# A state-space front rewritten: output tables as two products summed by TensorE, tables in the order of the rounds, eight modulation blocks moved behind it

## The chip, the cores and the metric

The kernel runs on one core of a Trainium2 chip. The metric is the device time of one execution in microseconds (us). The engines are TensorE (PE in the profile; PEld is its weight load), VectorE (DVE), ScalarE (ACT), GpSimd (POOL) and SyncE (SP), whose queue issues most of the DMAs.

## The reference

The input is one sequence of 512 tokens of width 1024 in float32, and a conditioning vector `c`. Four layers follow one another: a state-space mixer with a gated feed-forward, a short convolution with a gated feed-forward, dilated attention with a squared-ReLU feed-forward, and a gated recurrence with another. The change is in the first mixer and its surroundings:

```python
c_act = silu(c)
mods = c_act @ w_ada[i] + b_ada[i]              # 6 x 1024: sh1, sc1, g1, sh2, sc2, g2
h = rms_norm(x, norm1_g[i]) * (1 + sc1) + sh1
# 64 groups g of 16 channels, 64 complex states each
state_t = Abar_g * state_{t-1} + Bbar_g @ u_t   # Abar = exp((a_re + i a_im) * exp(log_step))
y_t = Re(C_g @ state_t) + D * u_t
x = x + g1 * (val * sigmoid(gate))              # [val, gate] = gelu(y) @ w_out
h = rms_norm(x, norm2_g[i]) * (1 + sc2) + sh2   # then the gated feed-forward
```

## The kernel before, in words

The first part, `s5()`, which this text calls the front, computes the mixer up to the GELU. A sequence of 512 tokens is cut into 64 chunks of 8. Inside a chunk the recurrence is a dense matrix, between chunks it is a scan. Everything is laid out by `f`, one of eight blocks of eight groups, and by `i`, one of four rounds of two blocks.

The front first makes, on VectorE, the discretised poles from `a_re`, `a_im` and `log_step` (arrays of 128 x 64), their powers 0 to 8 (`pre_`, `pim_`), and the scaled `B` (`b1`, `b2`) and `C` (`c1`, `c2`), the second of each pair being the first with its halves swapped by a matmul with a permutation (`io_matrices`). Then come tables. `tables(f)` makes `w1 = b1*pre_ + b2*pim_`, three VectorE operations of 128 x 1024, the middle one into `w1t` (for f = 1 and 4 on GpSimd); eight matmuls turn `w1` into `bt` (from inputs to chunk states) and into entries of `X`, the response inside a chunk. `out_tables(f)` makes `ft = c1*pre_ - c2*pim_`, from chunk states to outputs, in two halves of three GpSimd operations, with four buffers for `ft`.

A round `i` has these parts. `prep(i)` normalises the tokens into `U` and makes rotation factors `sr`, `cr` and the scan's decay `d0` (`sr` and `d0` on GpSimd for f < 5, on VectorE else). `states(i)` copies 16 groups of `X` into the block-triangular `TT` by eight DMAs on SP's queue, multiplies `U` by `bt` (L673), rotates, scans over 64 chunks (`tensor_tensor_scan`, L688), rotates back and writes `sp`, of which there are two buffers. `outs(i)` sums `U` by `TT` (L711) and `sp` by `ft` (L713) in PSUM, copies to `Y`, transposes, applies the GELU and splits the result into a rounded part `hhi` and a rest `hlo`.

Among these stand the first 20 of 24 blocks of layer 0's modulation: `ada` loads 1 MB of `w_ada` over SP into one of three `raw` buffers, and runs eight TensorE matmuls with `c_act` as weights (L241), a ScalarE copy, and two small matmuls (L247). The rest of the modulation, 4 blocks of layer 0 and 24 of layer 1, is done after the front by `ada_fill`: the same load, then one VectorE scaling (L277) and seven multiply-adds (L279), and for every four blocks a few small matmuls. These closures stand in a list, `fillers`; `pump()` runs one whenever the matmul loops `run` and `up` have loaded a weight block, 36 times up to the end of the convolution's input projection, where the rest is run at once.

The order of the front's parts is written by hand as a string of letters: T `tables`, O `out_tables`, P `prep`, S `states` (three steps), Y `outs` (two), A `ada`, K `setup` (token loads, `X`'s diagonal, identity copies), B `io_matrices`, Q and G scales and gains, Z and H pools. A scheduler assigns each engine's instruction order from the order of that program text and from when buffers come free; at run time each engine works in order.

After the front every matrix product runs as three float32r matmuls (L849 to L851): rounded weights by rounded input, rounded weights by the rest, rest of the weights by rounded input. `gain[0, 4]`, the second norm's factor `norm2_g * (1 + sc2)`, and `mod(0, 3)`, its shift, are read when the first projection is done, by `rms_to_h`.

Of the kernel before, what the change touches and what calls it, by code (L numbers as in the profile page):

```python
# [92 lines left out]
def body(ctx, tc, a, out):  # L93
# [275 lines left out]
    ORDER = ("A1 A1 K0 A1 A1 B0 T2 Q0 A1 Z0 O0 O4 A1 G0 T5 O2 T6 G1 T3 T0 A1 O1 A1 T1 P0 A1 T4 O5 O3 S0 A1 A1 "  # L369
             "P1 T7 A1 P2 S0 S1 S1 S0 Y0 H0 S2 A1 S2 S1 P3 A1 S2 Y0 O6 Y1 S3 A1 O7 S3 S3 A1 A1 Y1 Y2 Y2 Y3 Y3 "  # L370
             "A20")
    FA, FD = 5, 5

    def s5():

        def tiny(nm, n=64, pool=p1):
            return pool.tile([128, n], F32, name=nm)

        pt = pst("b")
# [49 lines left out]
        dt = exp(lg, "e0")  # L429
        mag = exp(tt(tiny("lrdt"), lr, dt), "e1")  # L430
        th = red2pi(tt(tiny("lidt"), li, dt), "t1")
# [9 lines left out]
        tt(pre_[:, 1, :], mag, cs)  # L441
        tt(pim_[:, 1, :], mag, sn)
        tmp = p1.tile([128, 4, 64], F32, name="pw_t")
        n = 1
        while n < 8:
            br = pre_[:, n:n + 1, :].to_broadcast([128, n, 64])
            bi = pim_[:, n:n + 1, :].to_broadcast([128, n, 64])
            src_r, src_i = pre_[:, 1:n + 1, :], pim_[:, 1:n + 1, :]
            dr, di = pre_[:, n + 1:2 * n + 1, :], pim_[:, n + 1:2 * n + 1, :]
            t = tmp[:, 0:n, :]  # L450
            tt(dr, src_r, br)
            tt(t, src_i, bi)
            tt(dr, dr, t, OP.subtract)
            tt(di, src_r, bi)
            tt(t, src_i, br)
            tt(di, di, t, OP.add)
            n *= 2
# [5 lines left out]
        V.reciprocal(den, den)  # L463
        am1 = tiny("am1")
# [13 lines left out]
        T2P = (1, 4)  # L478
        more = list(range(20))
# [10 lines left out]
        th8 = tiny("th8")  # L490
        V.tensor_scalar(th8, th, 8.0, None, op0=OP.mult)
        w8 = red2pi(th8, "t8")
        w8p = tiny("w8p", pool=pp)
        V.tensor_scalar(w8p, w8, 1.0 / (2 * math.pi), None, op0=OP.mult)
        w8 = w8p
        r8 = tiny("r8", pool=pp)
        tt(r8, mag, mag)
        tt(r8, r8, r8)
        tt(r8, r8, r8)


        b1, b2 = (pt1.tile([128, 64, 16], F32, name=nm) for nm in ("b1", "b2"))
        c1, c2 = (pp.tile([128, 64, 16], F32, name=nm) for nm in ("c1", "c2"))
        X = pp.tile([128, 64, 16], F32, name="X")
        TT = [pp.tile([128, 8, 16, 16], F32, name=f"TT{i}") for i in range(2)]
# [8 lines left out]
        def tables(f):  # L514
            g = slice(8 * f, 8 * f + 8)
            w1 = pt1.tile([128, 8, 8, 16], F32, name="w1", bufs=2)
            t2 = pt1.tile([128, 8, 8, 16], F32, name="w1t", bufs=1)
            tt(w1, b1[:, g, None, :].to_broadcast([128, 8, 8, 16]), bc(pre_, slice(0, 8), g))
            (P if f in T2P else V).tensor_tensor(t2, b2[:, g, None, :].to_broadcast([128, 8, 8, 16]),
                                                 bc(pim_, slice(0, 8), g), op=OP.mult)  # L520
            tt(w1, w1, t2, OP.add)
            ic = IC[f % 2]
            A.copy(ic[:, :, 128:144], c1[:, g, :])
            bt = pp.tile([128, 8, 128], F32, name=f"bt{f}")
            for g0, n in ((0, 3), (3, 3), (6, 2)):
                p = pst("c", (128, 3, 144))
                for j in range(n):
                    T.matmul(p[:, j], w1[:, g0 + j].rearrange("p l h -> p (l h)"), ic[:, g0 + j], start=True, stop=True)
                A.copy(bt[:, g0:g0 + n], p[:, 0:n, 0:128])
                gx = slice(8 * f + g0, 8 * f + g0 + n)  # L530
                tt(X[:, gx], X[:, gx], p[:, 0:n, 128:144], OP.add)
            Bt[f] = bt

        def out_tables(f):
            g = slice(8 * f, 8 * f + 8)
            ft = pp.tile([128, 8, 8, 16], F32, name="ft", bufs=4)
            for i in range(2):
                gs = slice(8 * f + 4 * i, 8 * f + 4 * i + 4)
                fi = ft[:, 4 * i:4 * i + 4]
                ft2 = pp.tile([128, 4, 8, 16], F32, name="ft2", bufs=1)  # L540
                P.tensor_tensor(fi, c1[:, gs, None, :].to_broadcast([128, 4, 8, 16]), bc(pre_, slice(1, 9), gs), op=OP.mult)
                P.tensor_tensor(ft2, c2[:, gs, None, :].to_broadcast([128, 4, 8, 16]), bc(pim_, slice(1, 9), gs), op=OP.mult)
                P.tensor_tensor(fi, fi, ft2, op=OP.subtract)  # L543
            Ft[f] = ft

        def io_matrices(_):
# [17 lines left out]
            for dst, src, tag in ((c2, c1, "a"), (b2, b1, "b")):  # L564
                for j in range(2):
                    p = pst(tag, (128, 32, 16))
                    T.matmul(fl(p), C("sw"), fl(src[:, hf[j]]), start=True, stop=True)
                    A.activation(dst[:, hf[j]], p, AF.Identity, scale=C("sg"))


        def setup(_):
            load_chunks()

            P.memset(X, 0.0)
            P.tensor_tensor(X[0:16], drow, C("e")[0:16, None, :].to_broadcast([16, 64, 16]), op=OP.mult)
            for ic in IC:
                A.copy(ic[:, :, 0:128], ident[:, None, :].to_broadcast([128, 8, 128]))
            for t in TT:
                P.memset(t, 0.0)

# [17 lines left out]
        def gains(h):  # L598
            ada_next(max(0, 4 * h + 4 - (20 - len(more))))
# [33 lines left out]

        def prep(i, st):
# [67 lines left out]
        def outs(i, st):  # L702
            U = st["U"]
            Y = ps2.tile([128, 8, 8, 16], F32, name="Y", bufs=1)
            for j in range(2):
                p = pst("c", (128, 4, 8, 16))
                for q in range(4):
                    gi = 4 * j + q
                    for s in range(2):
# [3 lines left out]
                        T.matmul(o, st["sp", s][:, gi, 0:64], Ft[2 * i + s][:, gi], start=False, stop=True,  # L713
                                 tile_position=(0, 64 * s))
# [24 lines left out]
        def open_h(_):  # L739
# [8 lines left out]
              "H": open_h, "B": io_matrices, "K": setup, "Q": token_scale, "G": gains, "Z": open_2}  # L748
# [10 lines left out]
    make_gain(0, 4, "norm2_g")  # L759
# [306 lines left out]

    ada_fill(0, 40, 48)
# [726 lines left out]
```

## Time and profile before

| | |
|---|---|
| median of 3 runs | 2768.0 us (2766.3 to 2771.34) |
| the profiled execution's own time | 2767.48 us |
| its span in the profile | 2765.7 us |
| mean granted TensorE clock | 0.989 of full speed |
| busy over the span | PE 2694.6, DVE 1565.3, ACT 1068.6, POOL 123.5 us |

The span runs from the first instruction to the last; 1.8 us of the time lie around it. An engine's busy time says how much it did, not whether anyone waited for it. Where the profile gives a stretch's granted clock, 1.00 stands for 2.4 GHz and 0.50 for 1.2 GHz.

### The profile page before, as it was taken

To read this page: it belongs to the slowest core of one execution; us is meant where nothing else is said; L and a number is where in the kernel's file an instruction comes from. 1 tells how busy PE (TensorE), PEld (TensorE's weight loads), DVE (VectorE), ACT (ScalarE), POOL (GpSimd) and SP (SyncE) were. 2 spreads that over 40 slices of the span, in tenths; PEclk is the share of its full clock that TensorE was granted. 3 is DMA by queue.
4 is the path that set the end of the run, shared out by engine and by line. 5 is a ranking of instruction groups with operands and counts; after the bars stand their busy time and mean duration, and the time that the engine had idled before them with its cause. 6 is when DMAs were issued, how large, how long until landed. Compare 5 with 4: busy or idle time off the path is not lost.

```text
span 2765.7 us, 37495 instructions
## 1 busy us (share of the span) xinstructions
PE 2694.6 (97%) x15356; PEld 2286.1 (83%) x15356; DVE 1565.3 (57%) x2803; ACT 1068.6 (39%) x1874; POOL 123.5 (4%) x123
## 2 busy tenths in 40 slices
PE   5889999999999999999999999999999999999998
PEld 3668988889889888898888888898888988988887
DVE  8767755547555333375555555664446766744436
ACT  4653422224334222254343344452323666432322
POOL 7420000000000000000000000000000000000000
PEclk8989999999999999999999999999999999999999
DMA  6547445432332233343332333222224212223221
GB/s 191 163 132 243 153 137 176 146 128 84 122 107 98 86 99 106 100 120 93 91 99 85 92 94 90 62 88 96 91 84 130 82 61 66 88 92 103 88 84 61
DMA packets 301008, 298.18 MB, mean 108 GB/s; under 512 B 9748, under 2 KB 287252, under 8 KB 300836
## 3 DMA queue, kind: packets, MB, share of 16 engines
q1 hardware_dynamic: 292660, 279.37, 31.4%
q10 hardware_dynamic: 5840, 10.05, 1.4%
q0 software_dynamic: 2336, 6.36, 1.0%
q8 instruction: 121, 1.98, 0.3%
q14 instruction: 51, 0.42, 0.0%
HBM read 278.71 MB, written 2.10 MB: 102 GB/s over the span
## 4 chain that ended last, share of the span: by engine, by line
PE 90%; DVE 4%; ACT 3%; DMA 1%; POOL 1%; issue 1%; SPq 0%; DVEq 0%; ACTq 0%; POOLq 0%
PE ps_mm L849 24%; PE ps_mm L850 24%; PE ps_mm L851 24%; PE ps_mm L862 2%; PE ps_mm L863 2%; PE ps_mm L864 2%; PE ps_sc L1322 1%; PE ps_pt L1349 1%; PE ps_b L673 1%; PE ps_mm L1224 1%; ACT whi L803 1%; POOL ft L543 1%; PE ps_mm L1226 1%; PE ps_x L241 1%; PE ps_mm L1225 1%
## 5 line engine op out<-in xcount | busy, mean ns | idle before, releaser
L849 PE MATMUL ps_mm<-hhi,whi 128*128 128x512 f32 (+1 forms) x2064 | 786.5, 381 | 0.0
L850 PE MATMUL ps_mm<-hlo,whi 128*128 128x512 f32 (+1 forms) x2064 | 782.6, 379 | 0.5 <-DVE hlo L359 0.5
L851 PE MATMUL ps_mm<-hhi,wlo 128*128 128x512 f32 (+1 forms) x2064 | 781.2, 378 | 0.5 <-DVE wlo L804 0.5
L803 ACT CAST whi<-raw 128x1024 fp32r<-128x1024 f32 (+1 forms) x428 | 414.0, 990 | 819.5 <-PE ps_mm L850 628.8
L804 DVE TENSOR_TENSOR wlo<-raw,whi 128x1024 fp32r<-128x1024 f32 (+1 forms) x428 | 485.4, 1151 | 380.6 <-ACT whi L803 350.4
L849 PEld LDWEIGHTS ps_mm<-hhi,whi 128*128 128x128 f32 x2064 | 387.8, 188 | 73.7 <-issue 3.1
L851 PEld LDWEIGHTS ps_mm<-hhi,wlo 128*128 128x128 f32 x2064 | 388.0, 188 | 72.6 <-DVE wlo L804 1.0
L850 PEld LDWEIGHTS ps_mm<-hlo,whi 128*128 128x128 f32 x2064 | 387.9, 188 | 70.4 <-DVE hlo L359 0.9
L850 PE MATMUL ps_mm<-hidl,whi 128*128 128x512 f32 (+1 forms) x1120 | 401.5, 359 | 0.0
L849 PE MATMUL ps_mm<-hidh,whi 128*128 128x512 f32 (+1 forms) x1120 | 401.3, 359 | 0.1
L851 PE MATMUL ps_mm<-hidh,wlo 128*128 128x512 f32 (+1 forms) x1120 | 400.8, 358 | 0.0
L850 PEld LDWEIGHTS ps_mm<-hidl,whi 128*128 128x128 f32 x1120 | 211.0, 188 | 31.2
L849 PEld LDWEIGHTS ps_mm<-hidh,whi 128*128 128x128 f32 x1120 | 210.3, 188 | 31.3 <-ACT hidh L358 0.3
L851 PEld LDWEIGHTS ps_mm<-hidh,wlo 128*128 128x128 f32 x1120 | 210.4, 188 | 31.0
L1172 DVE TENSOR_TENSOR xT<-xT,ps_mm 128x512 f32<-128x512 f32 (+1 forms) x128 | 71.7, 567 | 121.8 <-PE ps_mm L851 121.1
L862 PE MATMUL ps_mm<-hhi,whi 128*128 128x256 f32 x448 | 123.9, 281 | 1.0 <-ACT hq L1581 0.6
L863 PE MATMUL ps_mm<-hhi,wlo 128*128 128x256 f32 x448 | 124.4, 279 | 0.0
L864 PE MATMUL ps_mm<-hlo,whi 128*128 128x256 f32 x448 | 124.2, 280 | 0.2
L358 ACT CAST hidh<-silu 128x512 fp32r<-128x512 f32 (+1 forms) x124 | 68.9, 565 | 126.0 <-DVE silu L996 83.0
L957 DVE SCALAR_TENSOR_TENSOR xT<-ps_mm,mods,xT 128x512 f32<-128x512 f32 (+1 forms) x104 | 64.8, 625 | 92.6 <-PE ps_mm L851 92.5
L279 DVE SCALAR_TENSOR_TENSOR ada_acc<-raw,c_act,ada_acc 128x256 f32<-128x256 f32 x196 | 93.5, 483 | 4.9
L1273 POOL DMA_DIRECT2D qsw<-qc x48 | 23.4, 492 | 1564.4 <-ACT qc L1262 1550.5
(414 smaller groups left out, 3386.3 us busy)
## 6 DMA issues: line engine op xcount, KB each, us to landing
raw<-in_w_ada_dram SPq DMA_DIRECT2D x48, 1024.0 KB, 5.2
raw<-in_w_ffn_in_dram SPq DMA_DIRECT2D x44, 1024.0 KB, 4.9
raw<-in_ffn_w_up_dram SPq DMA_DIRECT2D x32, 1024.0 KB, 5.2
raw<-in_attn_w_in_dram SPq DMA_DIRECT2D x48, 512.0 KB, 4.7
raw<-in_ffn_w_down_dram SPq DMA_DIRECT2D x32, 768.0 KB, 4.3
raw<-in_w_ffn_out_dram SPq DMA_DIRECT2D x24, 768.0 KB, 4.3
raw<-in_conv_w_in_dram SPq DMA_DIRECT2D x12, 1024.0 KB, 5.0
raw<-in_attn_w_in_dram SPq DMA_DIRECT2D x12, 1024.0 KB, 4.8
```

Of the source, the lines that this page charges most:

```text
L279: V.scalar_tensor_tensor(ac, raw[:, k, :], c_act[:, k:k + 1], ac, op0=OP.mult, op1=OP.add)
L358: A.copy(hi, src)
L803: A.copy(hi[:, sl], raw[:, sl])
L804: V.tensor_tensor(lo[:, sl], raw[:, sl], hi[:, sl].bitcast(F32), op=OP.subtract)
L849: T.matmul(ps[:, 0:n], hi[:, k, cs], h, start=(k == 0), stop=False)
L850: T.matmul(ps[:, 0:n], hi[:, k, cs], l, start=False, stop=False)
L851: T.matmul(ps[:, 0:n], lo[:, k, cs], h, start=False, stop=(k == nk - 1))
L862: T.matmul(p[:, 0:n], hi[:, k, cs], h, start=(k == 0), stop=False)
L863: T.matmul(p[:, 0:n], lo[:, k, cs], h, start=False, stop=False)
L864: T.matmul(p[:, 0:n], hi[:, k, cs], l, start=False, stop=(k == nk - 1))
L957: V.scalar_tensor_tensor(x, ps, gcol[:, m:m + 1], x, op0=OP.mult, op1=OP.add)
L1172: V.tensor_tensor(x, x, ps, op=OP.add)
```

## The change

The output table of a block is kept as its two products `fa` and `fb`, two buffers each; the sign goes into `c2`, and TensorE sums by a second matmul on the same `sp`. GpSimd keeps only these 32 products, a small memset and copy, and one load. VectorE makes every `w1t` and `sr` and `X`'s diagonal, and clears `X` and `TT` first of all; ScalarE copies `d0`. The powers above the first become a step W of the order, after `io_matrices`, and small steps ahead of them change places. In the order, two tables precede round 0, and the others stand among the rounds. `ada` makes 12 blocks instead of 20; the eight for the second norm's shift and scale become fillers, ahead of all others, and the last of them makes `gain[0, 4]`.

```diff
-    ORDER = ("A1 A1 K0 A1 A1 B0 T2 Q0 A1 Z0 O0 O4 A1 G0 T5 O2 T6 G1 T3 T0 A1 O1 A1 T1 P0 A1 T4 O5 O3 S0 A1 A1 "
-             "P1 T7 A1 P2 S0 S1 S1 S0 Y0 H0 S2 A1 S2 S1 P3 A1 S2 Y0 O6 Y1 S3 A1 O7 S3 S3 A1 A1 Y1 Y2 Y2 Y3 Y3 "
-             "A20")
-    FA, FD = 5, 5
+    ORDER = ("A1 A1 B0 K0 A1 A1 W0 T0 Q0 T1 Z0 G0 P0 O0 S0 T2 A1 O1 S0 T3 A1 P1 S0 Y0 S1 O2 T4 A1 S1 T5 A1 G1 P2 O3 S1 "
+             "T6 T7 H0 Y0 Y1 S2 S2 P3 O4 A1 O5 S2 Y1 Y2 S3 A1 S3 O6 A1 O7 S3 Y2 Y3 A20 Y3")
...
+        X = pp.tile([128, 64, 16], F32, name="X")
+        TT = [pp.tile([128, 8, 16, 16], F32, name=f"TT{i}") for i in range(2)]
+        for t in (X, *TT):
+            V.memset(t, 0.0)
...
-        T2P = (1, 4)
-        more = list(range(20))
+        NADA = 12
+        more = list(range(NADA))
...
-            (P if f in T2P else V).tensor_tensor(t2, b2[:, g, None, :].to_broadcast([128, 8, 8, 16]),
-                                                 bc(pim_, slice(0, 8), g), op=OP.mult)
+            tt(t2, b2[:, g, None, :].to_broadcast([128, 8, 8, 16]), bc(pim_, slice(0, 8), g))
...
-            ft = pp.tile([128, 8, 8, 16], F32, name="ft", bufs=4)
+            fa, fb = (pp.tile([128, 8, 8, 16], F32, name=nm, bufs=2) for nm in ("fa", "fb"))
...
-                P.tensor_tensor(fi, c1[:, gs, None, :].to_broadcast([128, 4, 8, 16]), bc(pre_, slice(1, 9), gs), op=OP.mult)
-                P.tensor_tensor(ft2, c2[:, gs, None, :].to_broadcast([128, 4, 8, 16]), bc(pim_, slice(1, 9), gs), op=OP.mult)
-                P.tensor_tensor(fi, fi, ft2, op=OP.subtract)
-            Ft[f] = ft
+                P.tensor_tensor(fa[:, h], c1[:, gs, None, :].to_broadcast([128, 4, 8, 16]), bc(pre_, slice(1, 9), gs), op=OP.mult)
+                P.tensor_tensor(fb[:, h], c2[:, gs, None, :].to_broadcast([128, 4, 8, 16]), bc(pim_, slice(1, 9), gs), op=OP.mult)
+            Ft[f] = fa, fb
...
-            for dst, src, tag in ((c2, c1, "a"), (b2, b1, "b")):
+            for dst, src, tag, sign in ((b2, b1, "b", "sg"), (c2, c1, "a", "gs")):
...
-            P.memset(X, 0.0)
-            P.tensor_tensor(X[0:16], drow, C("e")[0:16, None, :].to_broadcast([16, 64, 16]), op=OP.mult)
+            V.tensor_tensor(X[0:16], drow, C("e")[0:16, None, :].to_broadcast([16, 64, 16]), op=OP.mult)
...
-            for t in TT:
-                P.memset(t, 0.0)
...
-            (P if f < FA else V).tensor_tensor(sr, w8[:, g][:, :, None].to_broadcast([128, 8, 64]),
+            V.tensor_tensor(sr, w8[:, g][:, :, None].to_broadcast([128, 8, 64]),
...
-                (P if 2 * i + s < FD else V).tensor_tensor(d0, r8[:, g][:, :, None].to_broadcast([128, 8, 64]),
-                                C("cm")[:, None, :].to_broadcast([128, 8, 64]), op=OP.mult)
+                A.copy(d0[:, :, 1:64], r8[:, g][:, :, None].to_broadcast([128, 8, 63]))
+                V.memset(d0[:, :, 0:1], 0.0)
...
-                        T.matmul(o, st["sp", s][:, gi, 0:64], Ft[2 * i + s][:, gi], start=False, stop=True,
-                                 tile_position=(0, 64 * s))
+                        for n, ft in enumerate(Ft[2 * i + s]):
+                            T.matmul(o, st["sp", s][:, gi, 0:64], ft[:, gi], start=False, stop=(n == 1),
+                                     tile_position=(0, 64 * s))
...
-    make_gain(0, 4, "norm2_g")
...
+    ada_fill(0, 24, 40)
+    last_fill = fillers.pop()
+    fillers.append(lambda: (last_fill(), make_gain(0, 4, "norm2_g")))
     ada_fill(0, 40, 48)
     ada_fill(1, 0, 16)
```

## Rows read from the trace of the kernel before

**Rows 1.** The page: the chain that ended last, by engine.

```profile
PE 90%; DVE 4%; ACT 3%; DMA 1%; POOL 1%; issue 1%; SPq 0%; DVEq 0%; ACTq 0%; POOLq 0%
```

**Rows 2.** Windows: stretch and length, then busy us (instructions) per engine, clock, DMA.

```profile
0.00:195.80 195.80, 145.25 (x1088) 102.85 (x1088) 145.97 (x255) 99.45 (x223) 99.02 (x71) 0.88 0.52 155
...
195.80:400.00 204.20, 203.09 (x1151) 175.16 (x1151) 148.61 (x269) 82.89 (x119) 0.00 (x0) 1.00 0.58 192
...
670.00:790.00 120.00, 120.00 (x621) 102.33 (x620) 60.08 (x96) 36.33 (x52) 0.00 (x0) 1.00 0.29 97
```

**Rows 3.** VectorE in time order: first loaded input, last of the front.

```profile
5.09 2.21 DVE L380 COPY arow<-arow 64x128 f32<-64x128 f32 x1 [4.01 <-DMA arow<-in_ssm_a_im_dram]
...
199.72 1.99 DVE L359 TENSOR_TENSOR hlo<-Y,hhi 128x1024 fp32r<-128x1024 f32 x1 [0.75 <-ACT hhi L358]
```

**Rows 4.** Windows: the same columns, inside the front.

```profile
84.30:201.70 117.40, 101.60 (x779) 72.09 (x778) 79.56 (x106) 67.65 (x147) 38.60 (x29) 0.88 0.45 143
...
28.70:201.70 173.00, 138.91 (x1038) 99.22 (x1037) 130.84 (x166) 93.83 (x211) 85.17 (x55) 0.86 0.44 144
```

**Rows 5.** TensorE in time order: start us, us, instruction.

```profile
84.28 0.41 PE L673 MATMUL ps_b<-U,bt 128*128 128x64 f32 x2
...
91.48 1.75 PE L673 MATMUL ps_b<-U,bt 128*128 128x64 f32 x14
...
111.37 0.45 PE L711 MATMUL ps_c<-TT,U 128*64 128x128 f32 x4
...
111.85 0.44 PE L711 MATMUL ps_c<-TT,U 128*64 128x128 f32 x4
...
129.42 7.09 PE L673 MATMUL ps_b<-U,bt 128*128 128x64 f32 x32 [4.54 <-DVE sp L426]
...
163.13 7.09 PE L673 MATMUL ps_b<-U,bt 128*128 128x64 f32 x32
```

**Rows 6.** VectorE groups, 28.7 to 201.7 us: busy us, mean ns, idle before.

```profile
L426 DVE TENSOR_TENSOR w<-w,w1t 128x1024 f32<-128x1024 f32 x8 | 14.1, 1761 | 3.7 <-POOL w1t L519 3.6
...
L519 DVE TENSOR_TENSOR w1t<-b,pw_im 128x1024 f32<-128x1024 f32 x6 | 11.5, 1924 | 0.1
...
L627 DVE TENSOR_SCALAR cr<-sr 128x512 f32<-128x512 f32 x8 | 8.8, 1135 | 0.0
...
L628 DVE SCALAR_TENSOR_TENSOR sr<-cr,sr 128x512 f32<-128x512 f32 x8 | 8.9, 1133 | 0.0
```

**Rows 7.** VectorE groups, 83 to 119 us, GpSimd nearly idle.

```profile
L426 DVE TENSOR_TENSOR w<-w,w1t 128x1024 f32<-128x1024 f32 x2 | 2.4, 1222 | 0.0
...
L519 DVE TENSOR_TENSOR w1t<-b,pw_im 128x1024 f32<-128x1024 f32 x1 | 1.2, 1215 | 0.0
...
L627 DVE TENSOR_SCALAR cr<-sr 128x512 f32<-128x512 f32 x2 | 0.8, 403 | 0.0
...
L628 DVE SCALAR_TENSOR_TENSOR sr<-cr,sr 128x512 f32<-128x512 f32 x2 | 1.4, 684 | 0.0
```

**Rows 8.** GpSimd groups of the front.

```profile
L543 POOL TENSOR_TENSOR ft<-ft,ft 128x512 f32<-128x512 f32 x16 | 27.7, 1734 | 0.9
...
L541 POOL TENSOR_TENSOR ft<-c,pw_re 128x512 f32<-128x512 f32 x16 | 21.8, 1380 | 24.7 <-PE ps_c L711 16.1 <-ACT c L556 5.1 <-PE ps_c L713 3.5
```

**Rows 9.** ScalarE in time order: one of two identity copies.

```profile
15.88 1.03 ACT L577 COPY IC<-cst_ident 128x1024 f32<-128x1024 f32 x1
```

**Rows 10.** VectorE's waits, 28.7 to 201.7 us: total us, times, longest.

```profile
DVE rb L426 <- PE ps_b L673: 16.2, 7, 4.5
...
DVE sp L426 <- issue: 7.1, 3, 3.8
...
DVE w L426 <- POOL w1t L519: 3.6, 1, 3.6
```

**Rows 11.** TensorE groups of the front: the modulation blocks.

```profile
L241 PE MATMUL ps_x<-raw,cz 128*32 128x256 f32 x320 | 27.6, 413 | 6.7 <-DVE mods L259 6.7
```

**Rows 12.** Instructions on `ada_acc`: duration min/median/max, first and last start.

```profile
L279 DVE SCALAR_TENSOR_TENSOR ada_acc<-raw,c_act,ada_acc x196: 472/485/488, 202.5 to 696.1; 128x256 f32<-128x256 f32 x196
```

More of the change, by code (lines that the diff above doesn't have):

```diff
@@ L429, in s5 @@
         dt = exp(lg, "e0")
+        th = red2pi(tt(tiny("lidt"), li, dt), "t1")
         mag = exp(tt(tiny("lrdt"), lr, dt), "e1")
-        th = red2pi(tt(tiny("lidt"), li, dt), "t1")
         sn, cs, ab = tiny("sn"), tiny("cs"), tiny("ab")
@@ L440, in s5 @@
         V.memset(pim_[:, 0, :], 0.0)
[L441 to L457, printed above, removed]
+        th8 = tiny("th8")
+        V.tensor_scalar(th8, th, 8.0, None, op0=OP.mult)
+        w8 = red2pi(th8, "t8")
+        w8p = tiny("w8p", pool=pp)
+        V.tensor_scalar(w8p, w8, 1.0 / (2 * math.pi), None, op0=OP.mult)
+        w8 = w8p
+        r8 = tiny("r8", pool=pp)
+        tt(r8, mag, mag)
+        tt(r8, r8, r8)
+        tt(r8, r8, r8)
         den, t1 = tiny("den"), tiny("tq")
@@ L463, in s5 @@
         V.reciprocal(den, den)
+        tt(pim_[:, 1, :], mag, sn)
+        tt(pre_[:, 1, :], mag, cs)
+        tmp = p1.tile([128, 4, 64], F32, name="pw_t")
         am1 = tiny("am1")
@@ L487, in fl @@
             return x.rearrange("p g h -> p (g h)")
[L490 to L499, printed above, removed]
         b1, b2 = (pt1.tile([128, 64, 16], F32, name=nm) for nm in ("b1", "b2"))
         c1, c2 = (pp.tile([128, 64, 16], F32, name=nm) for nm in ("c1", "c2"))
-        X = pp.tile([128, 64, 16], F32, name="X")
-        TT = [pp.tile([128, 8, 16, 16], F32, name=f"TT{i}") for i in range(2)]
         IC = [pt1.tile([128, 8, 144], F32, name=f"IC{i}") for i in range(2)]
@@ L535, in out_tables @@
             g = slice(8 * f, 8 * f + 8)
-            ft = pp.tile([128, 8, 8, 16], F32, name="ft", bufs=4)
+            fa, fb = (pp.tile([128, 8, 8, 16], F32, name=nm, bufs=2) for nm in ("fa", "fb"))
             for i in range(2):
-                gs = slice(8 * f + 4 * i, 8 * f + 4 * i + 4)
-                fi = ft[:, 4 * i:4 * i + 4]
-                ft2 = pp.tile([128, 4, 8, 16], F32, name="ft2", bufs=1)
-                P.tensor_tensor(fi, c1[:, gs, None, :].to_broadcast([128, 4, 8, 16]), bc(pre_, slice(1, 9), gs), op=OP.mult)
-                P.tensor_tensor(ft2, c2[:, gs, None, :].to_broadcast([128, 4, 8, 16]), bc(pim_, slice(1, 9), gs), op=OP.mult)
-                P.tensor_tensor(fi, fi, ft2, op=OP.subtract)
-            Ft[f] = ft
+                gs, h = slice(8 * f + 4 * i, 8 * f + 4 * i + 4), slice(4 * i, 4 * i + 4)
+                P.tensor_tensor(fa[:, h], c1[:, gs, None, :].to_broadcast([128, 4, 8, 16]), bc(pre_, slice(1, 9), gs), op=OP.mult)
+                P.tensor_tensor(fb[:, h], c2[:, gs, None, :].to_broadcast([128, 4, 8, 16]), bc(pim_, slice(1, 9), gs), op=OP.mult)
+            Ft[f] = fa, fb
         def io_matrices(_):
@@ L567, in io_matrices, with powers @@
                     T.matmul(fl(p), C("sw"), fl(src[:, hf[j]]), start=True, stop=True)
-                    A.activation(dst[:, hf[j]], p, AF.Identity, scale=C("sg"))
+                    A.activation(dst[:, hf[j]], p, AF.Identity, scale=C(sign))
+        def powers(_):
+            n = 1
+            while n < 8:
+                br = pre_[:, n:n + 1, :].to_broadcast([128, n, 64])
+                bi = pim_[:, n:n + 1, :].to_broadcast([128, n, 64])
+                src_r, src_i = pre_[:, 1:n + 1, :], pim_[:, 1:n + 1, :]
+                dr, di = pre_[:, n + 1:2 * n + 1, :], pim_[:, n + 1:2 * n + 1, :]
+                t = tmp[:, 0:n, :]
+                tt(dr, src_r, br)
+                tt(t, src_i, bi)
+                tt(dr, dr, t, OP.subtract)
+                tt(di, src_r, bi)
+                tt(t, src_i, br)
+                tt(di, di, t, OP.add)
+                n *= 2
         def setup(_):
             load_chunks()
-            P.memset(X, 0.0)
-            P.tensor_tensor(X[0:16], drow, C("e")[0:16, None, :].to_broadcast([16, 64, 16]), op=OP.mult)
+            V.tensor_tensor(X[0:16], drow, C("e")[0:16, None, :].to_broadcast([16, 64, 16]), op=OP.mult)
             for ic in IC:
                 A.copy(ic[:, :, 0:128], ident[:, None, :].to_broadcast([128, 8, 128]))
-            for t in TT:
-                P.memset(t, 0.0)
         def token_scale(_):
@@ L598, in gains @@
         def gains(h):
-            ada_next(max(0, 4 * h + 4 - (20 - len(more))))
+            ada_next(max(0, 4 * h + 4 - (NADA - len(more))))
             cs = slice(4 * h, 4 * h + 4)
@@ L747, in s5 @@
         do = {"T": tables, "O": out_tables, "P": lambda i: prep(i, sts[i]), "A": ada_next, "S": states_of, "Y": outs_of,
-              "H": open_h, "B": io_matrices, "K": setup, "Q": token_scale, "G": gains, "Z": open_2}
+              "H": open_h, "B": io_matrices, "K": setup, "W": powers, "Q": token_scale, "G": gains, "Z": open_2}
         for w in ORDER.split():
```

## The prediction, made before the changed kernel ran

> **What bounds the kernel now.** I read the chain of waits first: TensorE carries 90% of the chain that ended last [rows 1]. The windows say where it doesn't. From 195.8 us on, TensorE is busy without a break (203.1 of 204.2 us in the first stretch), and before that it is busy 145 of 195.8 us, at a granted clock of 0.88 [rows 2]. The first 196 us are the state-space front, which the change rewrites, and the rest is a queue of matmuls. So time saved in the front reaches the end one for one, time lost too, and work added behind 195.8 us costs only what it adds to TensorE. The profiled execution took 2767.48 us, 0.5 us under the median of 2768.0, so I count on its own time and the median is the same within a us.
>
> Which engine sets the pace of the front? From the first full-size VectorE operation at 28.7 us to the end of the last `hlo` at 201.7 [rows 3], VectorE is busy 130.8 of 173.0 us and TensorE 138.9 [rows 4]. TensorE's share has much in it that is only slow: its clock there is 0.86, and 32 of round 2's matmuls on `bt` take 7.09 us, where 14 in round 0 took 1.75, that is 4.0 for 32 [rows 5]. At full clock TensorE would have about 0.86 of its work, some 119 us. VectorE's is also inflated, by another thing: the same instruction takes 1.76 us on average in this stretch and 1.22 in 83 to 119 us, where GpSimd is nearly idle [rows 6, 7]. The chain through the front alternates between the two, and a step on one is late because the other is. I make the sum on VectorE, as busy time plus the 42.2 us in which it waits, and test it on the spacing of rounds.
>
> **The change, part by part.**
>
> *GpSimd's work.* Now 60 two-operand instructions run there while VectorE works: 16 each at L541, L543 and, of the same kind, L542, five `sr`, five `d0`, two `w1t` [rows 8]. Afterwards 32 remain: L543 goes, and the other twelve move. How much do they stretch VectorE? Sixteen `w` operations pay 0.54 us each (8.6; the eight that make the first product have the shape and count of the eight that add), six `w1t` 0.71 (4.3), eight `cr` 0.73 (5.9), eight `sr` roundings 0.45 (3.6): 22.4 us [rows 6, 7]. The rest of VectorE's work has some too; I take 30 in all, between 22.4 and 36. In proportion to the number of instructions, 28 of 60 take 14.0 us with them. Bounds: 0 if the 32 that stay all fall on a busy VectorE and cost as much as all do now, 22 if they fall in its pauses.
>
> The row: with GpSimd at work a VectorE product of two tables takes 1.76, without it 1.22 [rows 6, 7]. The Trainium skill ("SBUF — State Buffer", section "SBUF: two separate sides") says that the two engines share one port pair that is locked for a whole instruction, so the loser stands still for all of it. By that rule a GpSimd instruction met by VectorE costs its whole length, and the sum would lose up to its first term. The trace agrees that the two hinder each other; how much of the length is paid it leaves open.
>
> *Work that VectorE takes over.* Two `w1t` at 1.215 (2.4 us), five `sr` at 0.68, the quiet duration of a 128x512 operation (3.4), the diagonal of `X` at no more than 1.22 [rows 7]; three `d0` leave it (-2.0). Together +5.0. The three memsets also come to it, at the very start, where it now sits idle until 5.09 us for its first load and then copies for 2.21 us beside a busy GpSimd [rows 3]: 0 (without that cover, 5120 elements at 1.22 us per 1024, 6.2 us at most). `d0` becomes eight ScalarE copies of half the size of one that took 1.03 [rows 9], so under 8 us on an engine that is idle for 79 us of the stretch [rows 4]: 0.
>
> *The new order at the start.* `B` now stands ahead of `K`, so two ScalarE copies of 1.03 us [rows 9] no longer stand ahead of the copies of `b1`, on which TensorE and then VectorE wait: -2.0. The powers are moved behind the first products of `b`, where VectorE waited anyway. Bounds 0 and -7.
>
> *Tables in the rounds' order.* This is the largest term. Today all tables but one are made before the first round's matmuls at 84.28 [rows 5]; then VectorE is busy only 79.6 of 117.4 us [rows 4]. Afterwards two tables precede round 0, and the six others, 18 operations of 1.22 (22 us), stand among the rounds. The waits that they can fill or that go: 16.2 us for `bt`'s matmuls, 7.1 us at `sp` with no releaser named (a buffer of the two that the previous round's `Y` has not yet read; `Y` now stands ahead), 3.6 us for GpSimd's `w1t`, which is gone [rows 10]. I take all of the last two and half of the first: 42.2 - 18.7 = 23.5 us of waits left. Bounds: 38 left (only the `w1t` wait goes, to 3.6) and 7 left.
>
> *Two products on TensorE.* `Y` gets 64 more matmuls, two records each. Eight records (four of each kind) start within 111.85 - 111.37 = 0.48 us [rows 5], 0.06 each, so 128 cost 7.7 us, 1.9 a round. In the first three rounds they stand beside VectorE's work; in the last they are on the path: +1.9. Bounds 0 and 7.7. With two buffers for each product instead of four tables, the products of round i+1 wait for `Y` of round i, and `Y` of round i+1 for them: eight GpSimd instructions of 1.38 us, 11 us [rows 8], within a round of 26. Behind them on GpSimd stand only later products, so this costs 0; if it weren't covered, it would be the excess over the round.
>
> *Eight modulation blocks moved out.* In the front each issues one 1 MB load on SP, 16 records on TensorE (27.6 us over 20 blocks, so 1.4 each [rows 11]), a ScalarE copy, four small matmuls. They leave TensorE's work there (-11 us), which is not the pace, so 0 here, and leave SP's queue to the `TT` copies and the next weights. They come back as eight VectorE blocks of one scaling and seven multiply-adds of 0.485 [rows 12], some 3.8 us each. The queue of fillers shifts by eight: the projection after the front still has eight to run, and the surplus lands in the convolution, where VectorE is busy 60 of 120 us [rows 2] and gets up to 31 more. Each load takes one of three raw buffers on SP ahead of weights, as 28 such loads do today, beside a TensorE that is busy 120.0 of 120 us there. On TensorE they add two groups of small matmuls: +1.0 us. Bounds 0 and 5. If VectorE's cover fails in the convolution, the price is the surplus over its idle time, which is none.
>
> **The sum.** -14.0 + 5.0 - 2.0 - 18.7 + 1.9 + 1.0 = -26.8. 2767.5 - 26.8 = 2740.7 us.
>
> *The test on rounds.* Round 0 starts at 84.28 and round 3 at 163.13, 26.3 us apart on average, and from there to the end of `hlo` are 38.6 us [rows 3, 5]. Taking five tables, 15 stretched operations of 1.76, out of the way and 2 us at the start, round 0 would start near 55.9. A round of VectorE work is now (79.6 - 3.7 for the late table) / 4 = 19 us, with two tables 26.3. So 55.9 + 3 x 26.3 + 38.6 + 1.9 = 175, against 201.7: 26 us less, the sum's result within a us.
>
> **The rivals.**
>
> *A. The waits stay.* Each round is a chain of short steps that pass between VectorE and TensorE, and table work in between doesn't shorten it. For it: VectorE's longest waits are for TensorE's matmuls, not for lack of work [rows 10]. Against it: six tables are ready work with nothing before them. Only the `w1t` wait goes: -26.8 + 15.1 = -11.7, 2755.8 us.
>
> *B. Slower: tables stand in front of the rounds' steps.* VectorE works in order; a table's three operations ahead of a step keep TensorE waiting some 4 us, and after such a pause the clock is at half: round 2's 7.09 us came after 4.54 us without work [rows 5]. With fewer modulation blocks there is less to keep TensorE at work in between. A round would then cost 26.3 + 7.3 for tables + 3.1 for the slow matmuls on `bt` + 1.9 for `Y` + 1.9 for `Y` at half clock = 40.5: 55.9 + 121.5 + 40.5 = 217.9, 16 us more than now, 2785 us with the fills. It decides from a round of 35 us on. Against it: the longest spacing of today, round 2 to round 3 with its matmuls at half clock, is 33.7 us.
>
> *C. The port.* GpSimd's remaining 32 instructions cost VectorE as much as the 60 did. For it: 24 of them at L541's mean of 1.38 us [rows 8], fully blocking, are already 33 us; and they are now spread over the stretch in which VectorE is meant to be full. Against it: today's 60 cost only some 30. -26.8 + 14 = -12.8, 2754.7 us.
>
> *D. TensorE sets the pace of the front.* Then VectorE's gains are hidden, and what counts is -11 for the blocks, +7.7 for `Y`, +1: -2.3, 2765.2 us, no change that can be told. For it: 101.6 of 117.4 us busy from round 0 on [rows 4]. Against it: at the full clock an eighth of that would be gone.
>
> **How the numbers follow.** The forecast has 0.60, A 0.13, C 0.12, D 0.06, B 0.09. A measurement of this kernel tells about 0.2%, 5.5 us, from no change. So faster by over 0.2%: forecast, A and C, 0.85; within: D, 0.06; slower: B, 0.09. The likeliest case's own range is 2718 to 2752, from its bounds taken a few at a time (all at their best give 2767.5 - 22 + 5 - 7 - 35 = 2708). The range for 8 in 10 is 2715 to 2764: it takes in A and C and the lower end of the bounds, and leaves out B, most of D and a rest below 2715.
>
> **What would show it.** Right: the first long matmul at L849 starts near 169 us instead of 195.8; the front's VectorE share rises over 80% while its total falls to about 122 us between the same marks; `w` operations average about 1.5 us; the first matmuls on `bt` start near 56 us and rounds follow at 26 to 27. The convolution shows the `ada_acc` operations and a TensorE still full. Wrong: round spacing over 33 us, or `bt`'s matmuls at 7 us in every round (B); waits of VectorE for L673 as long as now (A); `w` at 1.76 or more (C); TensorE full from round 0 at full clock (D); or a TensorE with pauses between 600 and 800 us, where the moved blocks run.

## The result: 0.55% faster, and the profile after

The changed kernel takes 2753.0 us (median of 4 runs, 2751.6 to 2756.4) against 2768.6 for the kernel before beside it: a ratio of 0.9945, interval 0.9928 to 0.9962. That is faster by over 0.2%, inside the range, and 12 us above the predicted time: 15.6 us gained of a forecast 26.8.

The profiled execution took 2756.4 us, the longest of the four. Windows of the changed kernel, columns as in [rows 2], the first one from the mark of [rows 4] to its own last `hlo`:

```profile
28.70:176.70 148.00, 119.01 (x987) 90.18 (x985) 119.44 (x193) 92.87 (x209) 46.87 (x32) 0.88 0.32 103
...
195.80:400.00 204.20, 203.71 (x1159) 175.68 (x1158) 137.41 (x248) 75.60 (x112) 0.00 (x0) 1.00 0.52 171
670.00:800.00 130.00, 129.97 (x619) 106.69 (x619) 89.97 (x153) 40.15 (x53) 0.00 (x0) 1.00 0.54 177
```

The front ends at 176.7 us instead of 201.7 [rows 3], 25.0 earlier. VectorE is busy 119.4 us of it instead of 130.8 and waits 28.6 instead of 42.2 [rows 4]. The windows start at the same mark, but not at the same work: the powers' small operations, 5.6 us, stand behind the mark in the changed kernel and ahead of it in the kernel before. VectorE's groups there:

```profile
L428 DVE TENSOR_TENSOR w1t<-b,pw_im 128x1024 f32<-128x1024 f32 x8 | 12.2, 1528 | 0.1
...
L428 DVE TENSOR_TENSOR w<-w,w1t 128x1024 f32<-128x1024 f32 x8 | 11.3, 1417 | 0.1
...
L428 DVE TENSOR_TENSOR sp<-v,cr 128x512 f32<-128x512 f32 x8 | 8.9, 1117 | 0.0
...
L622 DVE SCALAR_TENSOR_TENSOR sr<-cr,sr 128x512 f32<-128x512 f32 x8 | 7.0, 910 | 0.0
...
L428 DVE TENSOR_TENSOR rb<-ps_b,sr 128x512 f32<-128x512 f32 x8 | 5.5, 690 | 9.4 <-PE ps_b L667 9.4
...
L621 DVE TENSOR_SCALAR cr<-sr 128x512 f32<-128x512 f32 x8 | 4.9, 645 | 0.0
```

Against [rows 6] `w` fell from 1761 ns to 1417, `cr` from 1135 to 645, and the wait for `bt`'s matmuls (L667 now) from 16.2 us [rows 10] to 9.4. TensorE in time order shows the starts of the rounds (at 60.17, 86.11, 104.74 and 144.90):

```profile
60.17 0.41 PE L667 MATMUL ps_b<-U,bt 128*128 128x64 f32 x2
...
86.11 3.79 PE L667 MATMUL ps_b<-U,bt 128*128 128x64 f32 x32
...
104.74 3.65 PE L667 MATMUL ps_b<-U,bt 128*128 128x64 f32 x16 [0.66 <-ACT U L646]
...
144.90 3.79 PE L667 MATMUL ps_b<-U,bt 128*128 128x64 f32 x32
...
178.46 0.79 PE L843 MATMUL ps_mm<-hhi,whi 128*128 128x512 f32 x1 [6.03 <-ACT whi L797]
```

In round 2, the third, 16 of these matmuls take 3.65 us, nearly as long as 32 in rounds 1 and 3. Their window has the granted clock (last column but two) at 0.50; the 32 at 86.11 and at 144.90 ran at 1.00:

```profile
104.70:112.30 7.60, 7.56 (x37) 7.59 (x38) 4.25 (x5) 6.43 (x19) 0.00 (x0) 0.50 0.48 156
```

The last row in time order is the first long matmul. In the kernel before, its counterpart (L849) started at 195.84, 5.9 us ahead of the end of the last `hlo`; now it starts 1.8 us behind it, after a wait of 6.0 us for the rounded weights. Behind this wait the granted clock is 0.50 from 178.5 to 182.5 us. ScalarE and SyncE's queue say why:

```profile
170.63 0.39 SPq L215 DMA_DIRECT2D raw<-in_ssm_w_out_dram  x1
```

```profile
172.83 1.91 ACT L358 CAST hhi<-Y 128x1024 fp32r<-128x1024 f32 x1
...
177.36 1.99 ACT L797 CAST whi<-raw 128x1024 fp32r<-128x1024 f32 x2
```

The load is issued only at 170.6: the three raw buffers hold the last modulation blocks and two sets of small vectors until then. How the lead runs on is read from the square root of each norm (L314 in both). First the kernel before, then the changed one:

```profile
L314 ACT ACTIVATE rs_s<-rs_v x2: 203/204/205, 279.2 to 295.4; 128x2 f32<-128x2 f32 x2
L314 ACT ACTIVATE rs_s<-rs_v x2: 203/203/203, 645.8 to 663.1; 128x2 f32<-128x2 f32 x2
L314 ACT ACTIVATE rs_s<-rs_v x2: 204/204/205, 825.5 to 842.8; 128x2 f32<-128x2 f32 x2
```

```profile
L314 ACT ACTIVATE rs_s<-rs_v x2: 203/204/205, 262.6 to 278.8; 128x2 f32<-128x2 f32 x2
L314 ACT ACTIVATE rs_s<-rs_v x2: 203/203/203, 630.0 to 647.3; 128x2 f32<-128x2 f32 x2
L314 ACT ACTIVATE rs_s<-rs_v x2: 203/204/204, 812.0 to 829.3; 128x2 f32<-128x2 f32 x2
```

The lead is 25.0 us at the last `hlo`, 17.4 at the first long matmul, 16.6 at the first norm, 15.8 ahead of the convolution, 13.5 behind it and 11.1 at the end. The last 2.4 us are within the scatter: from 812.0 to the end this execution took 1942.6 us, the kernel before 1940.2 from 825.5, and the same changed kernel profiled again 1938.9; over all traces of this study it is 1938.5 to 1942.6.

### The profile page after: what moved, and what is told of

It is laid out like the page before. It is cut to its first block, busy times and chain, and to the rows that moved or that the text cites. A ratio compares the mean times of both kernels' runs of the same rounds, so it can differ in the third digit from the quotient of the medians.

```text
span 2754.6 us, 37498 instructions
## 1 busy us (share of the span) xinstructions
PE 2686.2 (98%) x15344; PEld 2284.6 (83%) x15344; DVE 1578.5 (57%) x2883; ACT 1068.6 (39%) x1875; POOL 72.7 (3%) x91
## 4 chain that ended last, share of the span: by engine, by line
PE 90%; DVE 4%; ACT 4%; DMA 1%; issue 1%; SPq 0%; DVEq 0%; ACTq 0%
PE ps_mm L843 24%; PE ps_mm L844 24%; PE ps_mm L845 24%; PE ps_mm L856 2%; PE ps_mm L857 2%; PE ps_mm L858 2%; PE ps_sc L1319 1%; PE ps_pt L1346 1%; PE ps_mm L1221 1%; PE ps_mm L1223 1%; PE ps_mm L1222 1%; PE ps_st L323 1%; PE ps_b L667 1%; ACT whi L797 0%; PE ps_pv L1364 0%
## 5 line engine op out<-in xcount | busy, mean ns | idle before, releaser
L279 DVE SCALAR_TENSOR_TENSOR ada_acc<-raw,c_act,ada_acc 128x256 f32<-128x256 f32 x252 | 118.6, 483 | 5.2
L359 DVE TENSOR_TENSOR hidl<-silu,hidh 128x512 fp32r<-128x512 f32 (+1 forms) x124 | 75.9, 621 | 31.7 <-ACT hidh L358 29.8
```

What stands on the lines that cost most here:

```text
L279: V.scalar_tensor_tensor(ac, raw[:, k, :], c_act[:, k:k + 1], ac, op0=OP.mult, op1=OP.add)
L359: V.tensor_tensor(lo, src, hi.bitcast(F32), op=OP.subtract)
```

## The experiments

Theory H: the front became as short as forecast, and a third of it is lost at the hand-over to the projection. Rival F: the loss is inside the front. A second question is which part of the change shortened the front.

**The changed kernel again.** 

> The changed kernel once more, as the yardstick for the runs beside it: 2753 us, a ratio of 0.9945 to the kernel before within its interval of 0.9928 to 0.9962.

Measured: 2753.1 us, 0.9957 (0.9944 to 0.9969). The two medians agree within 0.1 us; over the kernel before that ran beside it the gain is 13.2 us here. In its trace the first table starts at 38.2 and the last `hlo` ends at 178.7, both 2 us later than above, and the wait at the hand-over is the same 6.0. So a mark inside the front moves by some 2 us from one execution to the next, and the losses behind it hardly do: 8.5 us of lead are gone by the first norm, 3.3 more behind the convolution.

**Small vectors out of the raw buffers.**

```diff
-        rt = raw_p.tile([128, 8, 256], F32, name="raw", tag="raw")[:, 0, 0:128]
-        load_rows(rt, rows, nc.sync)
+        rt = vt[i]
...
```

The two tiles `vt` are made and loaded in the step H of the order.

> The small column vectors that are loaded behind the front get two tiles of their own, loaded from SyncE's queue when the last round is prepared, instead of two of the three raw buffers. Theory H (the front became as short as forecast, 25 us, and a third of that is lost at the hand-over, where the first projection's weights wait for raw buffers): the first load of weights is issued two buffers earlier, near 156 us instead of 170.6, TensorE no longer waits 6.0 us for the first rounded weights, the first long matmul starts near 172.5 instead of 178.5, and the time falls by 6 to 8 us against the changed kernel, to about 2746. Rival F (the loss is inside the front, the last split ends at 176.7 and TensorE would only wait there): 0 to 2 us, 2751 to 2753.

Measured: 2751.9 us, 0.9947 (0.9935 to 0.996), about 1 us. The load is issued at 154.2 instead of 170.6, but the rounding of the weights stands behind the last `hhi` in ScalarE's queue; the first long matmul still waited 3.5 us. An early load alone doesn't settle the hand-over.

**Modulation blocks earlier.**

```diff
-... T5 A1 G1 P2 O3 S1 T6 T7 H0 Y0 Y1 S2 S2 P3 O4 A1 O5 S2 Y1 Y2 S3 A1 S3 O6 A1 O7 S3 Y2 Y3 A20 Y3
+... T5 A1 G1 A1 P2 A1 O3 S1 T6 T7 H0 A1 Y0 Y1 A1 S2 S2 P3 O4 O5 S2 Y1 Y2 S3 S3 O6 O7 S3 Y2 Y3 Y3
```

> The changed kernel, tables among the rounds as it has them, with the last four of the 12 modulation blocks done before the second round's outputs instead of during the last two rounds, so that the three raw buffers are free for the first projection's weights. Theory H (some 8 us of the front's gain are lost at the hand-over): the first rounded weights are there before the last hhi, TensorE's wait of 6.0 us for them goes, the first long matmul starts some 6 us ahead of the end of the last hlo as in the kernel before, and the time falls by 5 to 8 us, to 2745 to 2748, as with the tables first. Rival (the gain of tables first came from its tables and not from the hand-over): 0 to 2 us, 2751 to 2754.

Measured: 2746.8 us, 0.9932 (0.9919 to 0.9946), 6.3 under the changed kernel. The first weights are loaded at 141.0, and ScalarE rounds them ahead of the last `hhi`:

```profile
171.35 1.05 ACT L797 CAST whi<-raw 128x1024 fp32r<-128x1024 f32 x1
...
174.20 2.10 ACT L358 CAST hhi<-Y 128x1024 fp32r<-128x1024 f32 x1
```

```profile
172.80 0.50 PE L843 MATMUL ps_mm<-hhi,whi 128*128 128x512 f32 x1
```

The front ends at 178.3, 1.6 us later than in the changed kernel, and yet the first norm comes at 255.4 instead of 262.6. Theory H holds, and the other traces say the same. From the end of the last `hlo` to the first norm it takes 77.1 to 78.1 us in the seven in which the first long matmul starts over 5 us ahead of that end (the kernel before among them), and 84.2 to 88.1 in the seven in which it waited for its weights.

**Tables first.**

```diff
-... T0 Q0 T1 Z0 G0 P0 O0 S0 T2 A1 O1 S0 T3 A1 P1 S0 Y0 S1 O2 T4 A1 S1 T5 A1 G1 P2 O3 S1 T6 T7 H0 ...
+... T0 Q0 T1 Z0 G0 T2 T3 T4 T5 T6 T7 P0 O0 S0 A1 O1 S0 A1 P1 S0 Y0 S1 O2 A1 S1 A1 G1 P2 O3 S1 H0 ...
```

> All eight tables ahead of round 0, the rest of the changed order kept. The forecast's largest term (six tables among the rounds fill waits, -18.7, of which 3.6 is another wait that stays gone here): 15 us slower than the changed kernel, 2768, with VectorE's waits in the rounds back at some 38 us. Rival A (table work in between doesn't shorten the chain of a round): the same as the changed kernel within 3 us, 2750 to 2756. Rival B (tables in between hold up steps of rounds): 5 to 10 us faster than the changed kernel, 2745.

Measured: 2747.5 us, 0.9933 (0.9919 to 0.9946): 5.6 faster than the changed kernel where the forecast's term says 15 slower. VectorE's own order, which the scheduler makes, differs by three tables: in the changed kernel the last operations of the eight start at 43.5, 47.5, 56.1, 64.0, 69.8, 83.3, 107.4 and 114.3 us, here all by 74.6. Window, groups and a wait of this kernel, to its last `hlo`:

```profile
28.70:176.80 148.10, 120.62 (x1001) 89.32 (x999) 114.89 (x193) 96.57 (x213) 43.12 (x32) 0.91 0.33 107
```

```profile
L428 DVE TENSOR_TENSOR sp<-v,cr 128x512 f32<-128x512 f32 x8 | 5.4, 680 | 0.0
...
L621 DVE TENSOR_SCALAR cr<-sr 128x512 f32<-128x512 f32 x8 | 3.3, 416 | 0.0
...
L798 DVE TENSOR_TENSOR wlo<-raw,whi 128x1024 fp32r<-128x1024 f32 x2 | 2.5, 1225 | 7.4 <-ACT whi L797 7.4
...
L688 DVE MEMSET sp<- 128x8 f32 x8 | 0.5, 65 | 13.3 <-PE ps_c L708 13.3
```

The front is as long as with the tables among the rounds, 148.1 us. Without the two `wlo`, which belong to the projection, VectorE is busy 112.4 instead of 119.4 and idle 35.7 instead of 28.6. So tables among the rounds fill 7 us of waits and cost 7 us, because more of the rounds' own steps then run while GpSimd makes its products, from 126 to 137 us for one (`sp` 1117 ns against 680, `cr` 645 against 416). The 5.6 us come from the hand-over: the first long matmul starts at 171.3, 5.5 us ahead of the end of the last `hlo`.

**Products of two blocks only.**

```diff
         def out_tables(f):
+            if f > 1: Ft[f] = Ft[f % 2]; return
```

> GpSimd makes the two products only for the first two blocks (8 instructions instead of 32) and all later blocks use those; the output tables are wrong for six blocks and everything else is done as before. Forecast (0.5 us of VectorE per instruction of GpSimd): 24 instructions give 12 us in the front, of which the hand-over may hide up to 6: 2741 to 2747. Rival (they fall in VectorE's pauses and cost nothing): 2753. Rival C (GpSimd holds VectorE for its whole length, 24 x 1.38 us): 33 us in the front, 2720 to 2730.

The kernel leaves out the products of six blocks. Measured: 2742.9 us, 0.9917 (0.9904 to 0.9931), 10.2 under the changed kernel. Its window to its last `hlo`:

```profile
28.70:166.40 137.70, 116.95 (x987) 87.95 (x985) 109.00 (x194) 92.97 (x209) 14.75 (x8) 0.90 0.34 111
```

VectorE is busy 10.4 us less than in the changed kernel and idle 28.7, as there. 24 instructions cost 0.43 us each, against the forecast's 0.50.

**The kernel before, with one output table.**

```diff
         def out_tables(f):
+            if f > 0: Ft[f] = Ft[0]; return
```

> The kernel before, with its output table made on GpSimd for the first block alone and used for all eight (wrong output tables for seven blocks): 42 of GpSimd's 60 two-operand instructions are left out, nothing takes their place. Forecast's size (14.0 us for 28 instructions, 0.50 each): 21 us of VectorE's time in the front, 2746. The price that the run with two blocks' products showed in the changed kernel, 10.2 us for 24 or 0.43 each: 18 us, 2749. Rival C (a fixed cost that most instructions share, since VectorE only meets some of them): clearly less than 12 us, above 2755.

The kernel leaves out the output tables of seven blocks and uses the first block's for all. Measured: 2733.1 us, 0.9881 (0.9868 to 0.9895), 33 us faster than before and faster than any kernel of this study, the change included. Window to its last `hlo`, and two starts of rounds:

```profile
28.70:170.10 141.40, 125.98 (x1040) 88.48 (x1038) 110.75 (x165) 93.21 (x211) 25.37 (x16) 0.95 0.54 175
```

```profile
113.69 3.79 PE L673 MATMUL ps_b<-U,bt 128*128 128x64 f32 x32
...
135.93 3.79 PE L673 MATMUL ps_b<-U,bt 128*128 128x64 f32 x32
```

VectorE's busy time falls by 20.1 us, as forecast. Of the 42 instructions 39 stand in this window in the kernel before, so it is 0.52 each. What the expectation lacked are the waits: 42.2 becomes 30.6 with every table where it was. Of these 11.5 us, 3.6 are VectorE's wait for GpSimd's `w1t` [rows 10], which stood behind the output tables in GpSimd's queue; most of the rest are waits for TensorE. In [rows 5] the same matmuls took 7.09 us at half the clock, 1.2 GHz; here 3.79 at the full one, 2.4 GHz, and the front's mean granted clock is 0.95 instead of 0.86. First the window of the kernel before, then this one's:

```profile
129.40:136.50 7.10, 7.08 (x34) 6.96 (x35) 1.85 (x3) 5.01 (x9) 6.71 (x7) 0.50 0.19 66
```

```profile
113.70:117.50 3.80, 3.80 (x35) 3.73 (x36) 1.73 (x3) 3.80 (x9) 0.00 (x0) 1.00 0.65 180
```

Round 0's first matmuls start at 73.2 instead of 84.3, so 11 of the 31.6 us by which the front is shorter are gained ahead of the rounds.

**Blocks moved, alone, on the kernel before.** The edit is the change's `NADA = 12` and its fillers, with eight `A1` taken from the end of the order. 

> The kernel before with one part of the change alone: eight of the 20 modulation blocks leave the front and become fillers. Forecast (in the front TensorE's work is not the pace, so nothing is gained there, and the small matmuls of two more groups cost TensorE 1.0 us, or 2.3 as the changed kernel's convolution stage shows): 1 to 2 us slower than before. Rival D (TensorE sets the pace of the front, its 11 us come off): 9 to 10 us faster, a ratio near 0.9965. Third possibility: the hand-over changes, since fewer loads stand ahead of the first projection's weights: a few us either way, to be read from the start of the first long matmul.

Measured: 2771.5 us, 1.0014 (1.0005 to 1.0023), 4 us slower. From the norm ahead of the convolution (663.0) to the one behind it (828.3) this kernel takes 165.3 us; the kernel before 162.4, the changed one 164.7. Rival D's 9 to 10 us don't come: the front ends at 200.3, 1.4 us earlier. The run isn't a clean test of D's mechanism, though. With the blocks gone the front's granted clock is 0.80 instead of 0.86, which is what rival B said of fewer blocks, and how much of TensorE's 11 us that took back stays open.

**Blocks back in the front.** The change's fillers undone, eight `A1` spread over its order. 

> The changed kernel with the eight modulation blocks back in the front, spread over the order, and the list of fillers as in the kernel before. Forecast (they cost the front nothing and their small matmuls behind it 1.0 us, 2.3 as seen): 1 to 2 us faster than the changed kernel, 2751. Rival D (they load TensorE and SyncE's queue in the front with 11 us of work and eight more loads of 1 MB): 5 to 11 us slower, 2758 to 2764.

Measured: 2754.5 us, 0.9948 (0.9936 to 0.9961): no difference to the changed kernel that these runs can tell. The convolution's stretch is 162.5 us again, but TensorE still waits 6.0 us for the first weights. Rival D's 5 to 11 us don't appear. The front's granted clock is 0.93 instead of 0.88: the blocks load TensorE, and with them its clock is higher.

**The sine ahead of copies.**

```diff
+                with tc.issue_after(cs_i.ins): A.activation(fl(c1)[:, j * 512:(j + 1) * 512], ...)
...
+                with tc.issue_after(cs_i.ins): A.copy(ic[:, :, 0:128], ...)
```

> The changed kernel with the copies of c1 and of the identity issued on ScalarE behind the sine and cosine, nothing else moved. Theory S (the start is on VectorE's path, and its wait of 7.8 us for the sine is ScalarE standing in front of a copy that waits for a load): the wait shrinks to 1 us or less, the first table product starts near 29 instead of 36, and the time falls by 5 to 7.5 us to 2746 to 2748. Rival (another wait takes its place at the products with b, or later in the rounds): 0 to 2 us, 2751 to 2753.

Measured: 2754.1 us, 0.9948 (0.9936 to 0.9961), no gain that these runs can tell. The expectation was wrong: the wait only shrank, because a copy of the first modulation row, which waits for its own load, still stands ahead of the sine:

```profile
21.57 0.23 DVE L428 TENSOR_TENSOR pw_im<-e1q,sn 128x64 f32<-128x64 f32 x1 [4.75 <-ACT sn L435]
```

The first table starts at 33.6 instead of 36.0 and the profiled front ends 2.3 earlier, too little for these medians.

**Tables first and the sine.** 

> Tables first (2747.5 us) and the sine ahead of the copies together. If the start's wait is on the path there too: 5 to 7.5 us less, 2740 to 2742.5, faster than both kernels. Rival (rounds are paced by a chain that starts from elsewhere, such as the tokens' scale, or the hand-over gets its wait back): 2745 to 2748.

Measured: 2744.0 us, 0.9919 (0.9905 to 0.9933). The fastest of the kernels that leave nothing out: 9 us under the changed one, 23 under the kernel before.

**The same with rows behind the sine and the blocks back.** 

> Tables first, the sine ahead of the c1 and identity copies and of the first two modulation rows' copies, and the eight modulation blocks back in the front, among the tables and the rounds. The blocks behind the front cost 2.5 us in the convolution and 0.8 in the first feed-forward, and in the front the tables keep TensorE idle anyway: 3 us under the 2744 of tables first with the sine moved, and 2 to 4 more if VectorE's remaining wait for the sine (5.7 us) goes: 2737 to 2741. Rival (the eight loads stand ahead of the projection's weights or of the rounds' copies on SyncE's queue, or the copies that now come later hold the tables): 2744 to 2750.

Measured: 2752.0 us, 0.9949 (0.9935 to 0.9962), 8 slower than without these two edits. VectorE now waits 9.6 us for the products with `b` on TensorE, and the 6.1 us at the hand-over are back: its rival's way. The two edits weren't run apart.

**A round's first step ahead of the last outputs.**

```diff
-... P1 S0 Y0 S1 O2 A1 S1 A1 G1 P2 O3 S1 H0 Y0 Y1 S2 S2 P3 ...
+... P1 S0 S1 Y0 O2 A1 S1 A1 G1 P2 O3 S1 S2 H0 Y0 Y1 S2 P3 ...
```

> Tables first, the sine ahead of the copies and rows as in the run beside it, 12 modulation blocks, and in the order the first step of a round ahead of the previous round's outputs instead of behind them. If the rounds are paced by the chain of sp, the outputs' matmuls, and only then the next round's matmuls on bt (VectorE waits 13.3 us for the outputs and 7.2 for bt's matmuls with tables first): 5 to 12 us under 2744, 2732 to 2739. Rival (the two sp buffers or the clock after the longer queue of matmuls give the wait back elsewhere): 2741 to 2746.

Measured: 2756.5 us, 0.9969 (0.9956 to 0.9981), 12 slower than tables first with the sine. This kernel also has the modulation rows' copies behind the sine, as the one before it; its first table starts at 33.2 against 33.9 without, so the loss isn't there. TensorE now stands without work ahead of a round, and the matmuls then run slowly:

```profile
93.37 5.27 PE L667 MATMUL ps_b<-U,bt 128*128 128x64 f32 x32 [1.01 <-DVE sp L428]
...
117.51 7.09 PE L667 MATMUL ps_b<-U,bt 128*128 128x64 f32 x32 [3.90 <-DVE sp L428]
```

The windows of the pause and of the second row's matmuls give the clock:

```profile
113.60:117.50 3.90, 0.02 (x1) 0.00 (x0) 3.90 (x5) 1.23 (x2) 3.90 (x3) 0.79 0.75 219
117.50:124.60 7.10, 7.09 (x34) 6.97 (x35) 1.85 (x3) 7.04 (x10) 1.38 (x2) 0.50 0.21 73
```

TensorE did nothing for 3.9 us, and its granted clock is 0.50, 1.2 GHz, in the matmuls that follow. This is rival B's mechanism. The changed kernel has it too: TensorE stands without work for 4.4 us in round 2, and the granted clock from 136.4 to 141.6 us is 0.50:

```profile
136.40 1.97 PE L208 MATMUL ps_a<-cst_ident,raw 128*128 128x128 f32 x8 [4.39 <-ACT xT L210]
```

Ahead of the half clock at 104.7 there was no such pause: TensorE was busy 6.0 of the 9.0 us from 95 to 104, at 1.00. What else brings the clock down isn't shown here.

## Why the prediction was right in sign and half in size

*GpSimd's work and VectorE's, -14.0 + 5.0.* The price was right, the total in part by luck. Without the two `wlo` of the projection (2.5 us in the window of before, none in that of after) VectorE's busy time fell from 128.4 to 119.4, by 9.0. But 5.6 us of powers came into the window, so the same work fell by some 14 (an estimate from these numbers), and with tables first by 7 more. What the remaining 32 instructions cost depends on which steps of VectorE they meet, and a share of 28 in 60 can't say that. The price per instruction was 0.50 in the sum, 0.52 and 0.43 in the two runs that left them out. Rival C, in which the remaining 32 cost as much as 60, is refuted. The Trainium skill ("SBUF — State Buffer", section "SBUF: two separate sides") says that the loser stands still for a whole instruction; the 24 instructions left out were 32.1 us long (46.87 less 14.75) and cost VectorE 10.4, a third of it; in the kernel before it was 20.1 of 59.8 (85.17 less 25.37), a third too. The runs agree that there is a price and decide how much.

*Which engine sets the pace.* The prediction has VectorE and TensorE alternate. In the trace of the kernel before the chain that ended last runs through GpSimd's queue from 39.2 to 75.5 us: output tables, and behind them `sr`, `d0` and the `w1t` for which VectorE waits 3.6 us. [rows 1] gives GpSimd 1% of the whole span, and that 1% lies in the front.

*Tables among the rounds, -18.7.* The size was near: VectorE's idle time in the front, with the time of the two `wlo`, fell from 44.6 to 28.6, by 16. The cause was wrong. With tables first the idle time is 35.7 already, so 9 of the 16 came without the placing, and the 7 that the placing fills, contention takes: the front is as long. (The bound of 7 us left has no rows behind it: the waits that the term names add up to 26.9, which leaves 15.) Rival A said so much (table work in between doesn't shorten a round's chain), but expected the waits to stay. They go with GpSimd's instructions: leaving these out of the kernel before took 11.5 us of waits with no table among the rounds moved, TensorE's half clock there among them. For the change itself, which takes out 28 of 60 and moves the order too, that cause is argued, not shown.

*Start, -2.0.* Wrong sign: the first table starts at 36.0 instead of 34.0 (at 34.9 to 38.2 in the seven traces with this start, at 33.3 to 34.0 in the three with the start of before). VectorE waits 7.8 us for a sine that ScalarE had queued behind a copy waiting for its load; the sine ran at 14.05 us before and runs at 24.69 now:

```profile
24.96 0.23 DVE L428 TENSOR_TENSOR pw_im<-e1q,sn 128x64 f32<-128x64 f32 x1 [7.79 <-ACT sn L435]
```

The step looked at the copies that left the head of ScalarE's queue and not at those that came ahead of the sine.

*The front in all.* -25.0 measured, -27.8 from the terms of the front (without the modulation); the test on rounds said 175 for its end, measured 176.7. That this came within 2 us is luck: round 0 started 4.3 us later than the test said (60.2), the even spacing of 26.3 was wrong (25.9, 18.6, 40.2: 5.8 more in all), and from round 3 on it took 31.8 instead of 40.5. The long spacing is what rival B expected of every round (40.5), and in it the matmuls ran at half clock.

*The step that failed* is in the first paragraph: time saved in the front reaches the end one for one. It does only if the projection's weights come earlier too. The lead shrank from 25.0 to 16.6 by the first norm, 8.4 us: 7.6 until the first long matmul starts and the rest behind it, where the clock is at half at first. Finishing the modulation blocks early gave 6.3 back.

*Moved blocks, +1.0.* Mis-sized: +2.3 in the convolution and +0.8 in the feed-forward ahead of it (the lead falls from 16.6 to 15.8 to 13.5), 3.1 in all, within the bounds; alone, 4 us. The term left out the clock, which was lower without the blocks in both kernels (0.80 against 0.86, 0.88 against 0.93). That VectorE hides their 31 us was right: TensorE is busy 129.97 of 130.

## What to carry to other kernels

When the head of a kernel gets shorter, whatever its tail waits for must come earlier as well: look at which buffers hold up the next stage's first load, and at what stands ahead of its first operation in an engine's queue. Work put into an engine's waits is worth what it fills less what it suffers from the neighbours at work there, so its price is taken from rows with those neighbours. Of several edits made together, the plainest is tried alone: here the order of the tables, the largest term of the sum, gave the front nothing, as taking it back showed.

## What the runs showed of the hardware

GpSimd cost VectorE 0.43 to 0.52 us for each of its two-operand instructions, a third of their own length in both runs that left some out, and in the kernel before 11.5 us of waits came with that. Thirty-two matmuls of 128x64 took 3.79 us at a granted clock of 1.00 and 7.09 at 0.50, here after a TensorE without work for 3.9 us: that pause cost 3.3 us more than itself. With eight more modulation blocks in the front, 11 us of TensorE's work, the granted clock there was higher, 0.86 against 0.80 and 0.93 against 0.88.
